# An encoder layer on one core: the mixer starts with the values' projection, the gates ride on it

## The chip, the core and the metric

The kernel runs on one NeuronCore of a Trainium2 chip. The core has five engines that run side by side, each with its own queue of instructions: TensorE (PE; matrix products, with a separate row PEld for loading the stationary operand), VectorE (DVE), ScalarE (ACT), GpSimd (POOL) and SyncE (SP), which here issues the DMAs. An instruction starts when it is at the head of its engine's queue and what it waits for has come. Products land in PSUM, eight banks of 128 x 512 float32; everything else lives in SBUF. The metric is the time of one execution on the device in microseconds (us).

## What is computed

One layer over a sequence of 512 tokens with 1024 features, all float32: a gated feed-forward block (FFN), a mixer, a second FFN, each between two normalizations and added to the residual.

```python
def reference(x, ...):
    h = swiglu(rmsnorm(x, norm_ffn1_pre), w_ffn1_in, w_ffn1_out)
    x = x + 0.5 * rmsnorm(h, norm_ffn1_post)
    h = mixer(rmsnorm(x, norm_mix_pre), w_mix_in, ...)
    x = x + rmsnorm(h, norm_mix_post)
    h = swiglu(rmsnorm(x, norm_ffn2_pre), w_ffn2_in, w_ffn2_out)
    return x + 0.5 * rmsnorm(h, norm_ffn2_post)

def mixer(xn, w_in, ...):
    bg, cg, hc, q, k, v, o, ig, fg = jnp.split(xn @ w_in, split_points, axis=-1)
    y_conv = bg * (conv3(cg * hc) + conv_b)
    li = ig + gate_i_bias
    lf = log_sigmoid(fg + gate_f_bias)
    h = mlstm(q, k, v, li, lf) + flip(mlstm(flip(q), flip(k), flip(v), ...))
    y_mlstm = sigmoid(o) * headnorm(h)
    return concatenate([y_conv, y_mlstm]) @ w_out
```

`xn @ w_in` has these columns: three blocks of 512 for the convolution, 256 queries, 256 keys, 512 values, 512 output gates and 16 scan gates (an input and a forget gate for each of 4 heads and 2 directions). The mLSTM is evaluated in four chunks of 128 tokens, with running sums and maxima over the forget gates inside and across chunks.

## The kernel before

**Precision.** A float32 operand is split into a rounded part `hi` and a rest `lo` (`split`, L291: a cast on ScalarE, L292, and a subtraction, mostly on VectorE, L294). A product is three matmuls, hi\*hi, hi\*lo and lo\*hi. So a contraction over 1024 features, eight blocks of 128, is 24 matmuls. The larger products of the FFNs use a seven-product (Strassen) scheme.

**Buffers.** `bigt` gives wide tiles (128 x 4 x 516) out of a pool of 13, `wpool` split weights (12 tiles, that is six pairs), `rawp` four weights as loaded, `ps` the eight PSUM banks. The weights form one list, `stream`; `w_load` loads the next of it, `w_split` splits it, and `w_get(ahead)` hands out the oldest pair and has up to `ahead` more split.

**Order.** The program is written in Python and traced; a planner then sets the order of each engine's queue, from the order of the source as priority and from its own estimate of when inputs and buffers are there. `pin` and `queued` keep an instruction in the order of the source. `tc.issue_after(ins)` puts instructions of a block behind `ins` on the queue of that instruction's engine, with no wait of its own.

**Around the change.** The first FFN ends with a loop over four token blocks `tb`: the last five blocks of hidden columns are multiplied (`mm_out`, L589), then `finish1(tb, acc)` adds the residual (`post_norm`, L398 and L406) and normalizes for the mixer (`pre_norm`, L383). For blocks 2 and 3 it does both after block 3. `flip` (L387) transposes a normalized block on PE (L391) into `xT`, features by tokens, and splits it (four `bigt` tiles in all). `within1` flips blocks 0 and 1 in the loop, inside the multiplications of blocks 2 and 3. In the middle of the FFN's output product `wgates` (L696) loads the 16 gate columns and spreads them on GpSimd over a zeroed tile, 32 apart, as hi and lo (L700, L706, L707).

The mixer then runs in this order:

1. Five jobs of `mm_cols` (L422): the spread gates and the four tiles of queries and keys, first over tokens 0 to 255, with `flip(2)` before the third job and `flip(3)` within the fifth, then over tokens 256 to 511. All these are 256 columns wide. ScalarE scales and copies queries and keys to `qk`.
2. The scan gates' chain, `chain1` to `chain4` (L780 to L841), on VectorE and ScalarE with 36 rows in use, while PE makes three output gate tiles with `col()` (512 wide, 24 matmuls each); `gate_o` applies the sigmoid.
3. The keys' transposes `pkn` (L869), the last output gate tile, `conv(0)`, and the transposes `pn1` and `pn2` of the chain's results (L902 to L905), copied to `nat1` and `nat2`.
4. The values by token blocks (L959): 24 matmuls of 512 columns for each block, the block of `xT` as the stationary operand. After the first, `weigh_k` (L928) multiplies keys by decay factors into `kp`, and `weigh_q` (four matmuls L942, eight products L948) does so for the queries.
5. `head_a(0)` (L997, L1004), `states` (L977), and the heads, with convolution tiles among them; then the output projection (L1113) and the second FFN.

Of the kernel before, what the change touches and what calls it, by code (L numbers as in the profile page):

```python
# [37 lines left out]
def encoder_kernel(ctx: ExitStack, tc: tile.TileContext, a: dict, out: bass.AP):
# [239 lines left out]
    nc.gpsimd.memset(warm, 0.0)
# [18 lines left out]
    def rstd(parts, n, mul, tag="rs"):  # L297
# [12 lines left out]
        nc.gpsimd.tensor_tensor(out=r[:, 0:w], in0=acc, in1=nhalf[:, 0:w], op=ALU.pow)  # L310
# [383 lines left out]
    wg = {}  # L694

    def wgates():  # L696
        raw = small.tile([P, KD, 16], F32, tag="rawg", name="rawg", bufs=1)
# [4 lines left out]
        rv = raw.rearrange("p k (q h) -> p k q h", h=4)
        hv = hi.rearrange("p k (q h) -> p k q h", h=32)
        lv = lo.rearrange("p k (q h) -> p k q h", h=32)
        for q in range(4):
            nc.gpsimd.tensor_copy(out=hv[:, :, q, 0:4], in_=rv[:, :, q, :])  # L706
            nc.gpsimd.tensor_tensor(out=lv[:, :, q, 0:4], in0=rv[:, :, q, :], in1=f32(hv[:, :, q, 0:4]), op=ALU.subtract)  # L707
# [4 lines left out]
    def finish1(tb, acc):  # L712
# [29 lines left out]
    qk = bigt()  # L742
    nc.scalar.mul(qk[:, 0, 0:512], pq0, DK ** -0.5)
    nc.scalar.mul(qk[:, 1, 0:512], pq1, DK ** -0.5)
    nc.scalar.copy(qk[:, 2, 0:512], pk0)
    nc.scalar.copy(qk[:, 3, 0:512], pk1)


    RA, RB = bigt(), bigt()
    nc.gpsimd.memset(RA[0:36, 0:2], 0.0)  # L750
    I, F = RA[0:36, 0, 0:512], RA[0:36, 1, 0:512]
    T1, T2 = RA[0:36, 2, 0:512], RA[0:36, 3, 0:512]
    B, A = RB[0:36, 0, 0:512], RB[0:36, 1, 0:512]
# [402 lines left out]
```

## Time and profile before

| what | us |
|---|---|
| median of 3 runs (916.7 to 917.62) | 917.5 |
| the profiled execution | 914.88 |
| its span, first to last instruction | 913.1 |
| first FFN's input and output products end, on PE | 353.2 |
| first head matmuls (L997) on PE | 438.1 |
| output projection (L1113) begins on PE | 519.8 |

The profile is of one execution, and times within it are counted from the span's start. Rows of groups give line, engine, operation, output and input tile, shapes, count, then busy time and mean ns of one, then the engine's idle time just before them and what ended it. Rows of stretches give for each engine its busy time and count of instructions, then the granted PE clock, the share of the DMA engines in use and GB/s. Rows of the timeline give start, duration, engine, line, operation and count, with idle time before and its releaser in brackets. An instruction's duration on PE is longer than the distance to the next one, as matmuls are pipelined; prices of matmuls are therefore taken from stretches.

### The profile page before, as it was taken

The numbers are of one execution on the slowest core, as the hardware profiler recorded it, in microseconds if no ns is written. First come the engines' busy times: TensorE is split into PE (matmuls) and PEld (weight loads), VectorE is DVE, ScalarE is ACT, GpSimd is POOL, SyncE is SP. The second block draws the span as 40 slices with busy tenths as digits, with TensorE's granted clock in tenths as the row PEclk, the third lists the DMA queues.
The fourth block names the chain that finished last, engine by engine and source line by source line (L and its number), as shares of the span: only waits on it lengthen the run. The fifth ranks groups of instructions, "written<-read, shape, count | busy, mean of one in ns | idle before, by whom it ended". The sixth has DMA issues, their size and how long they took to land.

```text
span 913.1 us, 15007 instructions
## 1 busy us (share of the span) xinstructions
PE 900.1 (99%) x6015; PEld 816.9 (89%) x6015; DVE 690.5 (76%) x1116; ACT 462.2 (51%) x802; POOL 44.9 (5%) x67
## 2 busy tenths in 40 slices
PE   9999999999999999999999999999999999999997
PEld 7999999999877888988888888999999999977885
DVE  6988998888988359474566647889888988999435
ACT  7655555555456225481655435545545545566311
POOL 5000000000002001000011000000000000000000
PEclk9999999999999999999999999999999999999999
DMA  8234443343235614231422602224443432443402
GB/s 262 62 116 113 120 134 99 100 129 97 90 130 148 201 47 116 58 96 56 116 71 70 204 4 75 65 70 117 115 117 94 121 108 84 123 138 110 162 2 91
DMA packets 126256, 96.47 MB, mean 106 GB/s; under 512 B 4181, under 2 KB 114793, under 8 KB 126186
## 3 DMA queue, kind: packets, MB, share of 16 engines
q1 hardware_dynamic: 126186, 95.51, 34.8%
q8 instruction: 47, 0.77, 0.3%
q14 instruction: 23, 0.19, 0.1%
HBM read 93.40 MB, written 2.10 MB: 105 GB/s over the span
## 4 chain that ended last, share of the span: by engine, by line
PE 95%; DVE 2%; ACT 1%; issue 0%; DMA 0%; POOL 0%; DVEq 0%; POOLq 0%; SPq 0%; ACTq 0%
PE ps L431 43%; PE ps L589 14%; PE ps L422 12%; PE ps L564 10%; PE ps L453 5%; PE ps L1113 5%; PE ps L959 2%; PE ps L1028 1%; DVE big L294 1%; PE ps L343 1%; DVE wlo L294 1%; PE ps L391 0%; PE ps L1036 0%; DVE big L531 0%; PE ps L977 0%
## 5 line engine op out<-in xcount | busy, mean ns | idle before, releaser
L294 DVE TENSOR_TENSOR wlo<-raw,whi 128x1024 fp32r<-128x1024 f32 x207 | 245.1, 1193 | 68.0 <-ACT whi L292 49.8
L292 ACT CAST whi<-raw 128x1024 fp32r<-128x1024 f32 x211 | 211.7, 1028 | 133.1 <-DVE raw L158 46.4
L431 PE MATMUL ps<-big,whi 128*128 128x256 f32 x1920 | 265.0, 280 | 0.0
L431 PEld LDWEIGHTS ps<-big,whi 128*128 128x128 f32 x1920 | 243.5, 188 | 1.0 <-ACT whi L292 0.4
L431 PE MATMUL ps<-big,wlo 128*128 128x256 f32 x960 | 150.9, 280 | 0.0
L431 PEld LDWEIGHTS ps<-big,wlo 128*128 128x128 f32 x960 | 129.3, 188 | 0.0
L589 PE MATMUL ps<-whi,big 128*128 128x512 f32 x384 | 121.9, 395 | 0.2 <-ACT whi L292 0.2
L589 PEld LDWEIGHTS ps<-whi,big 128*128 128x128 f32 x384 | 72.1, 188 | 17.5 <-ACT whi L292 0.7
L422 PE MATMUL ps<-big,whi 128*128 128x512 f32 (+1 forms) x384 | 79.8, 358 | 0.0
L564 PE MATMUL ps<-whi,big 128*128 128x512 f32 x240 | 76.0, 395 | 2.6 <-ACT big L292 2.6
L589 PE MATMUL ps<-wlo,big 128*128 128x512 f32 x192 | 75.6, 395 | 0.0
L422 PEld LDWEIGHTS ps<-big,whi 128*128 128x128 f32 x384 | 63.5, 188 | 10.7 <-issue 0.2
L431 PE MATMUL ps<-big,ws 128*128 128x256 f32 x480 | 65.3, 280 | 0.0
L431 PEld LDWEIGHTS ps<-big,ws 128*128 128x128 f32 x480 | 60.3, 188 | 0.0
L564 PEld LDWEIGHTS ps<-whi,big 128*128 128x128 f32 x240 | 44.7, 188 | 13.5 <-ACT big L292 3.4
L501 ACT COPY t<-ps 128x256 f32<-128x256 f32 x40 | 14.9, 371 | 72.2 <-PE ps L431 72.0
L292 ACT CAST big<-big 128x512 fp32r<-128x512 f32 (+2 forms) x68 | 36.1, 581 | 23.2 <-DVE big L531 10.8
L564 PE MATMUL ps<-wlo,big 128*128 128x512 f32 x120 | 44.9, 393 | 0.0
L589 PEld LDWEIGHTS ps<-wlo,big 128*128 128x128 f32 x192 | 36.1, 188 | 8.4
L422 PE MATMUL ps<-big,wlo 128*128 128x512 f32 (+1 forms) x192 | 41.1, 356 | 0.0
L294 DVE TENSOR_TENSOR big<-big,big 128x512 fp32r<-128x512 f32 (+2 forms) x68 | 40.8, 638 | 0.1
L422 PEld LDWEIGHTS ps<-big,wlo 128*128 128x128 f32 x192 | 32.1, 188 | 5.5
(212 smaller groups left out, 1135.0 us busy)
## 6 DMA issues: line engine op xcount, KB each, us to landing
raw<-in_w_ffn_in_dram SPq DMA_DIRECT2D x88, 512.0 KB, 4.8
raw<-in_w_ffn_out_dram SPq DMA_DIRECT2D x44, 512.0 KB, 4.5
raw<-in_w_mix_in_dram SPq DMA_DIRECT2D x24, 512.0 KB, 4.5
raw<-in_w_mix_out_dram SPq DMA_DIRECT2D x8, 512.0 KB, 3.7
raw<-in_w_ffn_out_dram SPq DMA_DIRECT2D x10, 256.0 KB, 3.7
out_dram<-x SPq DMA_DIRECT2D x8, 256.0 KB, 2.0
x<-in_x_dram SPq DMA_DIRECT2D x4, 256.0 KB, 4.3
x<-in_x_dram SPq DMA_DIRECT2D x2, 512.0 KB
```

Source lines behind the costliest of these rows:

```text
L292: latest["hi"] = nc.scalar.copy(out=hi, in_=src)
L294: latest["lo"] = eng.tensor_tensor(out=lo, in0=src, in1=f32(hi), op=ALU.subtract)
L343: pin(nc.tensor.transpose(out=pt[:, blk(k)], in_=xs[:, blk(4 * b + k)], identity=ident))
L422: nc.tensor.matmul(o, ww[:, k, :], xk(xT, xx, k, sl), start=n == 0, stop=n == 3 * KD - 1)
L431: pin(nc.tensor.matmul(o, ww[:, k, :], x[xx][:, k, :], start=first and n == 0, stop=n == 11, skip_group_check=True))
L453: pin(nc.tensor.matmul(o, ww[:, k, :], xq_hl(xq, (k // 4, th))[xx][:, k % 4, :], start=n == 0, stop=n == 3 * KD - 1))
L501: nc.scalar.copy(a_[:, h1], x[:, h0])
L564: nc.tensor.matmul(acc[tb + t][half], left[n][x][:, blk(t)], right[n][y], start=first and x == y == 0, stop=last_ and x == 1, skip_group_c ...
L589: nc.tensor.matmul(acc[tb][half], hT[hh][:, blk(tb)], w[ww][:, blk(half, 512)], start=fresh and hh == ww == 0, stop=k == NF - 1 and hh == ...
L959: nc.tensor.matmul(pv_, xk(xT, xx, k, blk(tb)), ww[:, k % 2, :], start=n == 0, stop=n == 3 * KD - 1)
L1028: nc.tensor.matmul(dest[d][c], E[:, d * 512 + c * P:d * 512 + (c + 1) * P], vv[:, c, h, :], start=c % 2 == 0, stop=before[d][c] < 0, skip_ ...
L1113: nc.tensor.matmul(acc[half], yy[yi][:, k % 4, blk(tb)], wmo[k][wi][:, blk(half, 512)], start=(n == 0 and yi == 0 and wi == 0), stop=(n == ...
```

## The change

The order of the mixer's first half is turned around.

- The values come first, by token blocks, with the 16 gate columns appended: wide tiles grow to 528 columns (`BW`), each of four holding hi and lo of two feature blocks of 512 value and 16 gate columns. `v_split` fills them, through the new hook `prep`, just ahead of the FFN's last loop. Each block takes 24 matmuls of 256 and 24 of 272 columns into two banks. `flip(2)` and `flip(3)` stand halfway in the tiles of blocks 1 and 2.
- The gate columns of a block are copied, 32 apart, into `spread`, and four transposes bring them to the layout that the chain reads (`pg`). The zeroed wide tile of `wgates`, its GpSimd writes and the gates' 48 matmuls go; `wgates` only loads the raw columns.
- `finish1` handles block 2 before block 3.
- Queries and keys are four `col()` tiles 512 wide (`project`), among the steps of the chain; the first two weights' splits are queued behind the last flip's, and the chain's GpSimd memsets behind the last power function of the norms.
- Two output gate tiles follow within the chain, then `pkn`, `pn1` and `pn2`, the third output gate tile, `weigh_k`, the fourth, `weigh_q`, and `conv(0)`.
- Some constants share storage: the warm-up operand with the raw gates, `ones` with `vrows`, `parl` with a part of `QT` (filled by GpSimd).

```diff
@@ weights in the order of loading
         if w_in is w2i:
+            stream += [(wm[blk(i, 2 * P), V0:V0 + 512].rearrange("(k p) f -> p k f", p=P), 2) for i in range(4)]
             stream += [cols(wm, c) for c in (Q0, Q0 + P, K0, K0 + P)]
             stream += [cols(wm, O0 + i * P) for i in range(4)]
             stream += [cols(wm, CG)]
-            stream += [(wm[blk(i, 2 * P), V0:V0 + 512].rearrange("(k p) f -> p k f", p=P), 2) for i in range(4)]
@@ def ffn(...)
+        if prep:
+            prep()
         for tb in range(NT):
...
     def wgates():
-        raw = small.tile([P, KD, 16], F32, tag="rawg", name="rawg", bufs=1)
-        queued(raw, wm[:, GT:GT + 16].rearrange("(k p) f -> p k f", p=P))
-        gt = bigt(F32R).rearrange("p q f -> p (q f)")
-        nc.gpsimd.memset(f32(gt[:, 0:2048]), 0.0)
...
+        queued(rawg, wm[:, GT:GT + 16].rearrange("(k p) f -> p k f", p=P))
+
+    def v_split():
+        for i in range(4):
+            if not loaded:
+                w_load(1)
+            (raw,), _ = loaded.pop(0)
+            bt = bigt(F32R).rearrange("p q f -> p (q f)")
+            hi, lo = (bt[:, blk(n, 2 * BW)].rearrange("p (k f) -> p k f", k=2) for n in range(2))
+            split(hi[:, :, 0:512], lo[:, :, 0:512], raw.rearrange("p (k f) -> p k f", k=2))
+            rg = rawg[:, 2 * i:2 * i + 2, :]
+            nc.gpsimd.tensor_copy(out=hi[:, :, 512:BW], in_=rg)
+            nc.gpsimd.tensor_tensor(out=lo[:, :, 512:BW], in0=rg, in1=f32(hi[:, :, 512:BW]), op=ALU.subtract)
+            wv.append((hi, lo))
@@ def finish1(tb, acc)
-        for b in {0: (0,), 1: (1,), 2: (), 3: (2, 3)}[tb]:
+        for b in {0: (0,), 1: (1,), 2: (2,), 3: (3,)}[tb]:
@@ the mixer's beginning
-    pg, pq0, pq1, pk0, pk1 = pts = [ps() for _ in range(5)]
-    jobs = [wg[0]] + [w_get(min(2, 3 - i)) for i in range(4)]
-    hooks = {(2, 0): lambda: flip(2, st[2], xT), (4, 2): lambda: flip(3, st[3], xT)}
-    for half in range(2):
-        for i, (pt, w) in enumerate(zip(pts, jobs)):
-            mm_cols(pt[:, blk(half, 256)], w, xT, blk(half, 256), hooks if half == 0 else None, i)
...
+    for tb in range(NT):
+        pv_ = [ps(), ps()]
+        n = 0
+        for k in range(KD):
+            hi, lo = wv[k // 2]
+            if (tb, k) in ((1, 4), (2, 4)):
+                flip(tb + 1, st[tb + 1], xT)
+            for xx, ww in ((0, hi), (0, lo), (1, hi)):
+                for i, at in enumerate((slice(0, 256), slice(256, BW))):
+                    nc.tensor.matmul(
+                        pv_[i][:, 0:at.stop - at.start], xk(xT, xx, k, blk(tb)), ww[:, k % 2, at],
+                        start=n == 0, stop=n == 3 * KD - 1)
+                n += 1
+        for i in range(2):
+            nc.scalar.copy(vv[:, tb, 2 * i:2 * i + 2, 0:DV], pv_[i][:, 0:256].rearrange("p (h e) -> p h e", e=DV))
+        nc.scalar.copy(spread_v[:, tb, :, 0:4], pv_[1][:, 256:272].rearrange("p (q h) -> p q h", h=4))
+    pg = ps()
+    for tb in range(NT):
+        nc.tensor.transpose(out=pg[:, blk(tb)], in_=spread[:, blk(tb)], identity=ident)
+    mark.update(latest)
+    with tc.issue_after(mark["lo"].ins), tc.issue_after(mark["hi"].ins):
+        w_split(2)
+    with tc.issue_after(mark["pow"].ins):
+        RA, RB = bigt(), bigt()
...
@@ behind the definitions
+    def project(i):
+        pt = col()
+        nc.scalar.mul(qk[:, i, 0:512], pt, DK ** -0.5 if i < 2 else 1.0)
+
+    chain1()
+    project(0)
+    project(1)
+    chain2()
+    project(2)
+    project(3)
+    chain3()
+    po.append(col())
+    chain4()
+    po.append(col())
+    gate_o(0)
+    gate_o(1)
...
+    po.append(col())
+    gate_o(2)
+    weigh_k()
+    po.append(col())
+    gate_o(3)
+    weigh_q()
+    conv(0)
```

The transposes `pkn`, `pn1` and `pn2` with their copies are moved without a change, other than `parl`'s place; the values' loop of before (L959, 512 columns wide) is removed.

More of the change, by code (lines that the diff above doesn't have):

```diff
@@ L58, in bigt @@
     def bigt(dt=F32):
-        return big.tile([P, 4, 516], dt, tag="big", name=nm("big"))
+        return big.tile([P, 4, BW], dt, tag="big", name=nm("big"))
     def ps():
@@ L276, in encoder_kernel @@
     nc.gpsimd.memset(nhalf, -0.5)
-    warm = const.tile([P, 256], BF16, name="warm")
+    rawg = const.tile([P, KD, 16], F32, name="rawg")
+    warm = rawg.rearrange("p k f -> p (k f)").bitcast(BF16)
     nc.gpsimd.memset(warm, 0.0)
-    ones = const.tile([1, P], F32, name="ones")
+    vrows = const.tile([20, P], F32, name="vrows")
+    ones = vrows[0:1, :]
     nc.gpsimd.memset(ones, 1.0)
@@ L433, in mm_part, with ffn @@
                 n += 1
-    def ffn(xq, between, finish, mid=None, within=None, ahead=(2, 2, 1, 1), late=None):
+    def ffn(xq, between, finish, mid=None, within=None, ahead=(2, 2, 1, 1), late=None, prep=None):
         h = [bigt() for _ in range((NF + 3) // 4)]
@@ L742, in encoder_kernel @@
[L742 to L753, printed above, removed]
-    CM, U = RB[0:36, 2, 0:512], RB[0:36, 3, 0:512]
-    nc.gpsimd.memset(U, 1.0)
@@ L892, in conv @@
             split(yc[0][:, i, 0:512], yc[1][:, i, 0:512], acc)
-    po.append(col())
-    gate_o(3)
-    conv(0)
-    pn1, pn2 = ps(), ps()
-    pn2v = pn2[:, 0:256].rearrange("p (c r) -> p c r", r=64)
-    for c in range(NT):
-        nc.tensor.transpose(out=pn1[:, blk(c)], in_=Q1[:, blk(c)], identity=ident)
-    for c in range(NT):
-        nc.tensor.transpose(out=pn2v[:, c, 0:36], in_=Q2[:, blk(c)], identity=ident[0:36, 0:36])
-    nc.tensor.matmul(
-        pn2[:, 256:272], parl.rearrange("p e x -> p (e x)"), acd.rearrange("p q c -> p (q c)"),
-        start=True, stop=True,
-    )
-    Ct = bigt()
-    Cf = Ct.rearrange("p q f -> p (q f)")
-    Cs = Cf[:, 0:12 * 129].rearrange("p (q i e) -> p q i e", q=4, i=3)
-    nat1 = Cf[:, 1552:2064].rearrange("p (c r) -> p c r", r=P)
-    nc.scalar.copy(nat1, ch(pn1))
-    nat2 = const.tile([P, NT, 36], F32, name="nat2")
-    nc.scalar.copy(nat2, pn2v[:, :, 0:36])
-    acb = const.tile([P, 4, 4], F32, name="acb")
-    nc.scalar.copy(acb.rearrange("p q c -> p (q c)"), pn2[:, 256:272])
     kpt = bigt()
@@ L949, in weigh_q @@
             qt_pair[pr] = qt
-    wv = [w_get(min(2, 3 - i)) for i in range(4)]
-    for tb in range(NT):
-        pv_ = ps()
-        n = 0
-        for k in range(KD):
-            hi, lo = wv[k // 2]
-            for xx, ww in ((0, hi), (0, lo), (1, hi)):
-                nc.tensor.matmul(pv_, xk(xT, xx, k, blk(tb)), ww[:, k % 2, :], start=n == 0, stop=n == 3 * KD - 1)
-                n += 1
-        nc.scalar.copy(vv[:, tb, :, 0:DV], pv_.rearrange("p (h e) -> p h e", e=DV))
-        if tb == 0:
-            weigh_k()
-            weigh_q()
+    po = []
+    qk = bigt()
+    def project(i):
[13 more added lines that the diff above has]
+    gate_o(1)
+    pkn = [ps(), ps()]
+    for c in range(NT):
+        for pr in range(2):
+            nc.tensor.transpose(
+                out=pkn[c // 2][:, blk(2 * (c % 2) + pr)], in_=qk[:, 2 + pr, blk(c)], identity=ident,
+            )
+    pn1, pn2 = ps(), ps()
+    pn2v = pn2[:, 0:256].rearrange("p (c r) -> p c r", r=64)
+    for c in range(NT):
+        nc.tensor.transpose(out=pn1[:, blk(c)], in_=Q1[:, blk(c)], identity=ident)
+    for c in range(NT):
+        nc.tensor.transpose(out=pn2v[:, c, 0:36], in_=Q2[:, blk(c)], identity=ident[0:36, 0:36])
+    nc.tensor.matmul(
+        pn2[:, 256:272], parl, acd.rearrange("p q c -> p (q c)"),
+        start=True, stop=True,
+    )
+    Ct = bigt()
+    Cf = Ct.rearrange("p q f -> p (q f)")
+    Cs = Cf[:, 0:12 * 129].rearrange("p (q i e) -> p q i e", q=4, i=3)
+    nat1 = Cf[:, 1552:2064].rearrange("p (c r) -> p c r", r=P)
+    nc.scalar.copy(nat1, ch(pn1))
+    nat2 = const.tile([P, NT, 36], F32, name="nat2")
+    nc.scalar.copy(nat2, pn2v[:, :, 0:36])
+    acb = const.tile([P, 4, 4], F32, name="acb")
+    nc.scalar.copy(acb.rearrange("p q c -> p (q c)"), pn2[:, 256:272])
+    po.append(col())
[5 more added lines that the diff above has]
+    conv(0)
     ym = (bigt(F32R), bigt(F32R))
```

74 lines of the change are left out of this document (30 added, 44 removed).

## The prediction

> **What bounds the kernel now.** I read the page's busy times first, then the list of who waited for whom with TensorE (PE) as the waiting engine, then busy times by stretch of the mixer's beginning, and last the timeline around its one hole.
>
> ```profile
> PE 900.1 (99%) x6015; PEld 816.9 (89%) x6015; DVE 690.5 (76%) x1116; ACT 462.2 (51%) x802; POOL 44.9 (5%) x67
> ...
> PE 95%; DVE 2%; ACT 1%; issue 0%; DMA 0%; POOL 0%; DVEq 0%; POOLq 0%; SPq 0%; ACTq 0%
> ```
>
> The first line is busy time by engine, the second the chain that ended last. Both name PE, from its first matmul to its last. So a microsecond saved on another engine is worth nothing unless PE waits for it, and one of PE's queue is worth a microsecond. Where does PE wait?
>
> ```profile
> PE ps L564 <- ACT big L292: 2.6, 2, 1.3
> PE ps L285 <- POOL warm L278: 1.3, 1, 1.3
> PE ps L391 <- DVE t L383: 1.0, 1, 1.0
> ```
>
> (Total us, times, longest.) Of the longer waits only L391, the transposes of `flip`, lies in the stage that is changed. The stage in stretches that I cut at the borders between matmul groups:
>
> ```profile
> core 0: us, PE busy (x) PEld busy (x) DVE busy (x) ACT busy (x) POOL busy (x), PEclk, DMA share, GB/s
> 353.17:358.84 5.67, 5.67 (x49) 5.61 (x47) 5.46 (x11) 3.20 (x9) 0.30 (x1) 1.00 0.81 229
> 358.84:360.02 1.18, 0.15 (x2) 0.03 (x1) 0.89 (x2) 0.00 (x0) 0.77 (x2) 1.00 0.96 234
> 360.02:370.74 10.72, 10.72 (x90) 10.37 (x90) 5.51 (x11) 3.60 (x8) 3.81 (x7) 1.00 0.08 29
> 370.74:384.95 14.21, 14.21 (x122) 14.21 (x121) 8.14 (x11) 5.37 (x7) 0.00 (x0) 1.00 0.18 43
> 384.95:401.63 16.68, 16.68 (x74) 13.47 (x73) 13.45 (x23) 14.16 (x17) 0.62 (x2) 1.00 0.42 124
> 401.63:402.43 0.80, 0.80 (x9) 0.79 (x8) 0.77 (x2) 0.79 (x1) 0.00 (x0) 1.00 0.15 26
> 402.43:413.61 11.18, 11.18 (x51) 9.05 (x50) 4.14 (x6) 9.02 (x13) 0.00 (x0) 1.00 0.41 115
> 413.61:414.71 1.10, 1.10 (x11) 0.90 (x9) 0.84 (x1) 0.90 (x2) 0.00 (x0) 1.00 0.81 243
> 414.71:438.12 23.41, 23.41 (x101) 18.72 (x100) 10.86 (x18) 5.50 (x10) 0.00 (x0) 1.00 0.11 30
> ```
>
> The reader should see that PE is full (clock 1.00) in every row but the second. In order the rows are: gates and first query tile over tokens 0 to 255; the hole; the two late flips and the rest of that half; the same five jobs over tokens 256 to 511; three output gate tiles; key transposes; the fourth gate tile and `conv(0)`; transposes of the decay factors; the values with `weigh_q`'s four matmuls in them. The counts take in instructions that straddle a border, so matmuls are counted from the code. The prices: a narrow matmul (256 columns) in the fourth row, 5 x 24 of them, is 14.21 / 120 = 0.1184 us. A wide one (512) in the fifth, 3 x 24, is 16.68 / 72 = 0.2317 us. A transpose in the sixth is 0.80 / 8 = 0.10 us.
>
> **Part by part.**
>
> *Gates' own projection goes.* 24 narrow matmuls for each half of the tokens, 48 x 0.1184 = 5.68 us, all on PE's path. **-5.68.**
>
> *Values narrow instead of wide.* Before: 96 wide, 23.41 - 4 x 0.2317 for `weigh_q` = 22.48 us. After: 96 of 256 columns and 96 of 272 (16 gate columns behind the values). No row has 272 columns. Between the two prices a column costs (0.2317 - 0.1184) / 256 = 0.00044 us, so 272 cost 0.1184 + 16 x 0.00044 = 0.1255 us. Ends: 0.1184 (the columns hide behind the weight load) and 0.2317 (as the next wider row). I take 0.1255, since 272 is sixteen columns from the first row and 240 from the second. 96 x 0.1184 + 96 x 0.1255 = 23.42 us. **+0.94**, with ends of +0.25 and +11.1.
>
> *Queries and keys wide instead of narrow.* 192 x 0.1184 = 22.73 against 96 x 0.2317 = 22.24. **-0.49.**
>
> *Gates turned.* Gates now come out by tokens, so four transposes of `spread` are added, 4 x 0.10. **+0.40.** They wait for ScalarE's three copies out of the last value tile. From the nearest rows:
>
> ```profile
> L501 ACT COPY t<-ps 128x256 f32<-128x256 f32 x40 | 14.9, 371 | 72.2 <-PE ps L431 72.0
> ...
> 414.99 0.18 ACT L917 COPY acb<-ps 128x16 f32<-128x16 f32 x1
> ```
>
> 2 x 0.37 + 0.18 = 0.92 us. If the first query tile's matmuls (24 x 0.2317 = 5.6 us, needing only `xT` and a split weight) stand ahead of the transposes on PE's queue, this is hidden. If not, some 1 us shows. Ends 0 and 1.0; I take **+0.3**. Queued behind them is all of PE.
>
> *The hole.* It is the wait for block 2's norm:
>
> ```profile
> 347.76 1.22 DVE L294 TENSOR_TENSOR wlo<-raw,whi 128x1024 fp32r<-128x1024 f32 x1
> ...
> 351.79 1.22 DVE L294 TENSOR_TENSOR wlo<-raw,whi 128x1024 fp32r<-128x1024 f32 x1
> ...
> 355.92 1.22 DVE L294 TENSOR_TENSOR wlo<-raw,whi 128x1024 fp32r<-128x1024 f32 x1
> ...
> 359.13 1.41 DVE L383 SCALAR_TENSOR_TENSOR t<-x,rs,gb 128x512 f32<-128x512 f32 x2 [0.39 <-POOL rs L310]
> ...
> 364.17 1.42 DVE L383 SCALAR_TENSOR_TENSOR t<-x,rs,gb 128x512 f32<-128x512 f32 x2 [0.73 <-POOL rs L310]
> ```
>
> Five weight splits (three shown) of queries, keys and the first output gate stand on VectorE's (DVE) queue among the norms of blocks 2 and 3, whose last steps are the L383 rows. After the change PE has value tiles of blocks 0 and 1 first. A tile is 24 x 0.1184 + 24 x 0.1255 = 5.85 us, so `flip(2)`, halfway in tile 1, is due at 353.17 + 5.85 + 2.93 = 361.95, and `flip(3)` after two more half tiles and one flip, at 368.6. Even at today's times the norms end at 360.5 and 365.6, 1.4 and 3.0 us earlier. The query splits also leave that place (they are queued behind the last flip), and block 2's norm is issued one block earlier. **-1.03** (1.18 less 0.15 busy). What is late next is the last flip's own split:
>
> ```profile
> L292 ACT CAST whi<-raw 128x1024 fp32r<-128x1024 f32 x211 | 211.7, 1028 | 133.1 <-DVE raw L158 46.4
> ...
> L294 DVE TENSOR_TENSOR big<-ps,big 128x512 fp32r<-128x512 f32 x24 | 15.6, 684 | 16.1 <-ACT big L292 16.1
> ...
> L292 ACT CAST big<-ps 128x512 fp32r<-128x512 f32 x24 | 13.5, 588 | 25.9 <-PE ps L343 15.3 <-PE ps L391 10.3
> ```
>
> Cast 0.59 and subtract 0.68 for each half stand against 2.9 us of matmuls between the flip and its first reader. (The first row is the cast of a weight, used below.)
>
> *What moves off PE.* The values' four splits go ahead of the FFN's last blocks, one cast and one subtract each:
>
> ```profile
> 306.60:346.60 40.00, 40.00 (x178) 32.42 (x177) 19.00 (x33) 10.52 (x24) 2.20 (x4) 1.00 0.27 81
> ...
> 283.48 2.04 POOL L706 CAST big<-rawg 128x32 fp32r<-128x32 f32 x4 [12.27 <-DMA rawg<-in_w_mix_in_dram]
> 285.48 3.27 POOL L707 TENSOR_TENSOR big<-rawg,big 128x32 fp32r<-128x32 f32 x4
> 332.44 0.55 POOL L310 TENSOR_TENSOR rs<-rs,nhalf 128x1 f32<-128x1 f32 x1 [43.69 <-DVE rs L306]
> ...
> 306.61 132.69 SPq L147 DMA_DIRECT2D raw<-in_w_mix_in_dram  x22
> ...
> raw<-in_w_mix_in_dram SPq DMA_DIRECT2D x24, 512.0 KB, 4.5
> ```
>
> DVE is busy 19.0 of these 40 us, and gets 4 x 1.22 = 4.9 more. GpSimd keeps its four casts and four subtracts of the same size, 5.3 us in an idle stretch of 43.69. Without that cover a norm's power function would queue behind them and its flip come up to 5.3 us late. The four value loads take the queries' places on SP's queue; at 4.5 us each one after another they land by 306.6 + 18 = 325, and are read at 353. The other loads keep their count. `weigh_k` and `weigh_q` keep their instructions and have two column tiles and `conv(0)` as cover where they had three value tiles. I cost all this at nothing. The VectorE copy of `parl` and one GpSimd memset, off the path, go for nothing as well.
>
> *Sum:* -5.68 + 0.94 - 0.49 + 0.40 + 0.3 - 1.03 = -5.56, say **-5.6 us**. The profiled execution took 914.88 us, so 909.3; the median of the runs shown is 917.5, 2.6 above it, and so 911.9 is my time.
>
> **A rule weighed.** The row says 0.1184 us for 256 columns and 0.2317 for 512: by the column nearly the same. The Trainium skill, TensorE: Matmul & The Clock Gate, section "Back-to-back issue gap", gives for streams of loads and matmuls about 81 ns at 128 columns and 131 ns at 512, which makes wide ones much cheaper by the column. An estimate on that line, 98 ns at 256 and 100 at 272, makes the values 96 x 0.131 = 12.6 us before and 19.0 after, +6.4 instead of +0.94, and the change no gain. The trace disagrees with it at 512 columns (231.7 ns against 131).
>
> **Rivals.**
>
> *A hole stays at the mixer's start* (-2.6, 914.9 us). There are 13 wide buffers. By the code's lifetimes the FFN's last blocks hold five (two for sums, three for hidden columns), `xT` four, and the values' weights now four: exactly 13. If the fourth weight must wait for the FFN's sums, last read here,
>
> ```profile
> 357.65 0.68 DVE L398 TENSOR_TENSOR t<-big,gb 128x512 f32<-128x512 f32 x1
> ```
>
> it is split at 358.3 + 1.03 + 1.22 = 360.6, while PE wants it after 36 matmuls, at 357.6: 3.0 us lost. For it: no buffer is spare. Against: VectorE frees those sums earlier without the splits.
>
> *It doesn't do what it says* (917.5). The queue order isn't the source's but comes from a planner with estimated times. If PE's queue has a group ahead of a flip or of the gates' transposes that in truth comes later, waits like the 1.03 us recur, and some five of these eat the gain. For it: the hole before is such a wait. Against: in 85 us there is just one.
>
> *The gate chain ends last* (slower). The gates' scan runs on VectorE and ScalarE from the first row here to the end of the second, and the third reads its result:
>
> ```profile
> 379.09 3.04 DVE L783 TENSOR_SCALAR big<-ps,gbias 4x512 f32<-4x512 f32 x4
> ...
> 405.50 1.40 DVE L834 TENSOR_TENSOR big<-big,big 4x512 fp32r<-4x512 f32 x2 [1.64 <-ACT big L833]
> ...
> 413.61 0.60 PE L902 MATMUL ps<-ident,big 128*128 128x128 f32 x4
> ```
>
> 27.8 us, with 6.7 to spare. Afterwards gates exist only when the last value tile is done: 353.17 + 23.4 + two flips and a small transpose 1.8 = 378.4, copies and transposes to 379.7. PE then has six column tiles (33.4), and key transposes: the reader is due at 378.4 + 0.4 + 33.4 + 0.8 = 413.0. Spare 5.5. Each us of chain beyond 33.3 costs one; from 38.9 on the change is slower. At 41 it is +2.1: 919.6. Against: the splits per column tile stay, and the sigmoids, which stood within the chain, are now issued behind it.
>
> *Narrow matmuls paced by their loads* (slower). PEld's mean is 188 ns for each load; were that the pace, 192 x (0.188 - 0.122) = +12.7, net +7.1: 924.6. Against: the first stretch has 48 narrow ones, each with its load, in 5.67 us. The skill's rule above would also end on this side.
>
> **How the numbers follow.** Forecast 0.64, hole 0.17, no effect 0.08, chain 0.08, load pace 0.03. The best case is 272 columns at the price of 256 and no wait for the copies, -5.56 - 0.68 - 0.3 = -6.5 (911.0), and the three runs of before differ by 0.9 us; low end 909.6. The upper end has to reach past the hole's 914.9 with the same scatter: 916.2. That leaves out the last three cases, 0.19. This kernel's measurement tells about 0.2% (1.8 us) from no change; faster than that are the forecast and the hole, 0.81; the same 0.08; slower 0.11.
>
> **What would show it.** Right: no 256-column `L422` matmuls in the mixer; value tiles at about 5.85 us each; no PE wait for L383 near 360; PE's first head matmuls (438.1 before) near 432.5, and everything behind shifted by that. Wrong: value tiles over 6.5 us (272 columns dear); PE idle before the gates' transposes over 1 us; a PE wait for a flip, or for a value weight's split; PE idle ahead of the transposes of the decay factors (chain). The forecast falls if the stretch to the first head matmul shrinks by 5.6 us but a later one grows.

## The result and the profile after

The changed kernel takes 911.0 us (median of 6 runs, 909.44 to 911.71) against 916.78 of the kernel before, run beside it (6 runs, 914.57 to 917.62): a ratio of 0.9938, with a 95% interval of 0.9927 to 0.995. That is 5.78 us less, where 5.56 had been worked out. Its profiled execution took 911.16 us.

The page after, with the busy times by engine and the chain that ended last:

```profile
PE 896.4 (99%) x5971; PEld 814.5 (90%) x5971; DVE 691.1 (76%) x1115; ACT 460.2 (51%) x807; POOL 42.5 (5%) x68
...
PE 91%; DVE 4%; DMA 2%; ACT 1%; issue 1%; DVEq 0%; POOLq 0%; POOL 0%; ACTq 0%
```

PE is still the bound, with 44 matmuls fewer: 48 of the gates are gone and four transposes have come. The list of PE's waits after (total us, times, longest):

```profile
PE ps L567 <- ACT big L295: 2.7, 2, 1.3
PE ps L567 <- ACT wt L295: 2.0, 2, 1.0
PE ps L288 <- POOL rawg L280: 1.3, 1, 1.3
PE ps L592 <- ACT whi L295: 0.4, 2, 0.2
PE ps L434 <- ACT whi L295: 0.2, 1, 0.2
```

The wait for block 2's norm is not among them (the transposes of `flip` are now L394), and none of these is in the mixer. The wait for `wt` was one of 0.9 us before; it lies in the first FFN's output product and is taken up below. The mixer's first stage, cut at the borders between groups of matmuls:

```profile
core 0: us, PE busy (x) PEld busy (x) DVE busy (x) ACT busy (x) POOL busy (x), PEclk, DMA share, GB/s
356.51:365.25 8.74, 8.74 (x74) 8.73 (x73) 6.61 (x14) 3.56 (x11) 3.48 (x6) 1.00 0.01 3
365.25:366.04 0.79, 0.79 (x11) 0.79 (x9) 0.00 (x0) 0.16 (x1) 0.79 (x2) 1.00 0.00 0
366.04:381.69 15.65, 15.65 (x132) 15.65 (x130) 8.13 (x9) 8.28 (x15) 1.11 (x3) 1.00 0.31 84
381.69:382.17 0.48, 0.48 (x6) 0.28 (x4) 0.40 (x1) 0.14 (x1) 0.00 (x0) 1.00 1.15 299
382.17:415.76 33.59, 33.59 (x146) 27.17 (x146) 22.97 (x35) 22.75 (x31) 0.62 (x2) 1.00 0.47 125
415.76:417.74 1.98, 1.98 (x19) 1.78 (x17) 1.23 (x1) 1.06 (x2) 0.00 (x0) 1.00 0.27 79
417.74:428.96 11.22, 11.22 (x49) 9.13 (x49) 3.30 (x7) 3.16 (x6) 0.00 (x0) 1.00 0.33 93
428.96:429.89 0.93, 0.93 (x5) 0.75 (x4) 0.67 (x1) 0.60 (x1) 0.00 (x0) 1.00 0.00 0
429.89:435.56 5.67, 5.67 (x25) 4.33 (x24) 5.52 (x9) 1.05 (x1) 0.00 (x0) 1.00 0.34 95
```

The rows are: 72 value matmuls; `flip(2)`; 120 value matmuls with `flip(3)` and one of the gates' transposes; two more of these and a small one of L875; six column tiles with the fourth gates' transpose; key transposes and those of the chain's results; two output gate tiles; `weigh_q`'s matmuls; `conv(0)`. In all nine PE is busy as long as the stretch lasts. The stage took 79.05 us, from the end of the FFN's products at 356.51 to the first head matmul at 435.56; before it was 353.17 to 438.12, 84.95 us. **5.90 us are gone from this stage**, and the prediction's 5.56 had named this stage alone.

The spans of the two profiled executions (913.1 and 909.4) differ by 3.7 only, because they started differently. The first matmul of the first FFN ran at 10.75 us in the one before and at 13.70 in the one after. Other runs of both families began at times between these two, so lengths of stages are compared from here on, and not instants.

### The profile page after: what moved, and what is told of

The parts are those of the page before. It is cut to its first block, busy times and chain, and to the rows that moved or that the text cites. A ratio compares the mean times of both kernels' runs of the same rounds, so it can differ in the third digit from the quotient of the medians.

```text
span 909.4 us, 14920 instructions
## 1 busy us (share of the span) xinstructions
PE 896.4 (99%) x5971; PEld 814.5 (90%) x5971; DVE 691.1 (76%) x1115; ACT 460.2 (51%) x807; POOL 42.5 (5%) x68
## 4 chain that ended last, share of the span: by engine, by line
PE 91%; DVE 4%; DMA 2%; ACT 1%; issue 1%; DVEq 0%; POOLq 0%; POOL 0%; ACTq 0%
PE ps L434 39%; PE ps L592 13%; PE ps L425 12%; PE ps L567 9%; PE ps L456 5%; PE ps L1133 5%; PE ps L755 3%; DMA raw<-in_w_ffn_in_dram 2%; DVE big L297 1%; DVE wlo L297 1%; PE ps L346 1%; PE ps L1048 1%; DVE big L534 1%; ACT big L295 1%; PE ps L288 1%
## 5 line engine op out<-in xcount | busy, mean ns | idle before, releaser
L297 DVE TENSOR_TENSOR wlo<-raw,whi 128x1024 fp32r<-128x1024 f32 x203 | 240.0, 1192 | 49.3 <-ACT whi L295 25.7
L295 ACT CAST whi<-raw 128x1024 fp32r<-128x1024 f32 x207 | 207.4, 1029 | 123.6 <-DVE raw L159 48.1
L434 PEld LDWEIGHTS ps<-big,whi 128*128 128x128 f32 x1920 | 243.0, 188 | 1.2 <-ACT whi L295 0.7
L434 PEld LDWEIGHTS ps<-big,wlo 128*128 128x128 f32 x960 | 129.5, 188 | 0.0
L425 PE MATMUL ps<-big,whi 128*128 128x512 f32 x320 | 78.3, 397 | 0.0
L567 PE MATMUL ps<-whi,big 128*128 128x512 f32 x240 | 75.2, 392 | 2.7 <-ACT big L295 2.7
L425 PEld LDWEIGHTS ps<-big,whi 128*128 128x128 f32 x320 | 59.5, 188 | 13.7 <-issue 0.2
L567 PEld LDWEIGHTS ps<-whi,big 128*128 128x128 f32 x240 | 44.7, 188 | 12.9 <-ACT big L295 3.5
L567 PE MATMUL ps<-wlo,big 128*128 128x512 f32 x120 | 44.6, 391 | 0.0
L425 PE MATMUL ps<-big,wlo 128*128 128x512 f32 x160 | 40.4, 395 | 0.0
L425 PEld LDWEIGHTS ps<-big,wlo 128*128 128x128 f32 x160 | 30.0, 188 | 7.0
```

Source lines behind the costliest of these rows:

```text
L295: latest["hi"] = nc.scalar.copy(out=hi, in_=src)
L297: latest["lo"] = eng.tensor_tensor(out=lo, in0=src, in1=f32(hi), op=ALU.subtract)
L425: nc.tensor.matmul(o, ww[:, k, :], xk(xT, xx, k, sl), start=n == 0, stop=n == 3 * KD - 1)
L434: pin(nc.tensor.matmul(o, ww[:, k, :], x[xx][:, k, :], start=first and n == 0, stop=n == 11, skip_group_check=True))
L567: nc.tensor.matmul(acc[tb + t][half], left[n][x][:, blk(t)], right[n][y], start=first and x == y == 0, stop=last_ and x == 1, skip_group_c ...
```

## The experiments

My theory was the prediction's sum: less work in PE's queue and one hole closed. Against it stood four rivals: that the new order of the queue is all that counts, that some buffer or norm holds PE at the start, that the gate chain sets the end, and that the mixed widths cost or save something else. All stage lengths below are read from the traces, between the same two matmuls as above. A kernel that was timed several times has its ratio to the kernel before with its interval; of the others, timed once, only the stages are compared (kernels that left the stage's work alone gave 79.05 to 79.06 in four executions).

| kernel | first FFN, us | stage, us | heads, us | second FFN to the end, us | time, us |
|---|---|---|---|---|---|
| before | 342.42 | 84.95 | 81.68 | 346.17 | 916.78 |
| after | 342.81 | 79.05 | 81.53 | 345.30 | 911.0 |
| e1_flip_later | 341.52 | 83.72 | 81.67 | 346.36 | 915.67 |
| e2_gates_one_product | 341.63 | 84.68 | 81.68 | 347.37 | 917.17 |
| e3_norms_late | 341.91 | 79.06 | 81.53 | 345.23 | 909.61 |
| e4_qk_halves | 342.84 | 79.37 | 81.53 | 345.27 | 910.8 |
| e5_values_512_and_16 | 342.60 | 88.49 | 81.53 | 345.23 | 917.37 |
| e6_one_more_wide_tile | 342.20 | 79.06 | 81.53 | 345.23 | 910.43 |
| e7_gates_not_riding | 342.55 | 78.50 | 81.54 | 345.23 | 907.79 |
| e8_chain_longer | 342.80 | 88.67 | 81.52 | 345.21 | 920.58 |
| e11_chain_half | 343.47 | 79.54 | 81.53 | 345.26 | 911.97 |
| e9_before_row528 | 341.07 | 85.06 | 81.81 | 345.17 | 915.2 |
| e10_after_row532 | 344.33 | 78.95 | 81.24 | 346.87 | 913.87 |
| again | 342.88 | 79.06 | 81.53 | 345.29 | 910.55 |

### The hole, closed by itself in the kernel before

```diff
-    hooks = {(2, 0): lambda: flip(2, st[2], xT), (4, 2): lambda: flip(3, st[3], xT)}
+    hooks = {(3, 0): lambda: flip(2, st[2], xT), (4, 2): lambda: flip(3, st[3], xT)}
```

> The kernel before, with the flip of block 2 ahead of the fourth of the five narrow jobs instead of the third, so that PE has 24 more narrow matmuls (2.84 us) ahead of it. My theory (two terms: PE work removed, and the hole of 1.03 us closed): PE's wait for L383 near 360 us goes, and the stretch from the end of the FFN's products to the first head matmuls shrinks from 84.95 to about 83.9 us; the time falls by 1.0 us. Rival (the gain is all one of order, of norms and flips that come earlier): about 5 us less, near 80 us. Second rival (a wait only moves): 84.95 stays, with PE waiting elsewhere in the stretch.

The stage shrank from 84.95 to 83.72, by 1.23, and the ratio is 0.9988 [0.9979, 0.9998]. The wait for L383 is not in its list of waits any more:

```profile
PE ps L564 <- ACT big L292: 2.6, 2, 1.3
PE ps L285 <- POOL warm L278: 1.3, 1, 1.3
PE ps L564 <- ACT wt L292: 0.9, 1, 0.9
```

So one more query job ahead of the flip covers the norm, and the hole was worth a fifth of the change. The rival that closing it is all the change does falls: 4.7 us of the stage are left to explain.

### The gates' matmuls, a third of them kept

```diff
...
-        for ww, xx in ((hi, 0), (hi, 1), (lo, 0)):
+        for ww, xx in ((hi, 0), (hi, 1), (lo, 0))[:terms]:
...
@@ the mixer's beginning
-            mm_cols(pt[:, blk(half, 256)], w, xT, blk(half, 256), hooks if half == 0 else None, i)
+            mm_cols(pt[:, blk(half, 256)], w, xT, blk(half, 256), hooks if half == 0 else None, i, 3 if i else 1)
```

This is the kernel before with the gates computed from hi\*hi alone: 32 matmuls leave, 32 x 0.1184 = 3.79 us.

> The kernel before, with the gates' projection cut to its first product (hi*hi, 16 of 48 narrow matmuls; the two other products of the gates are left out). My theory: PE work falls by 32 x 0.1184 = 3.79 us, but 16 of these matmuls were cover for the flip of block 2, so the hole grows by up to 1.9 us, from 1.0 to about 2.9; the stretch shrinks from 84.95 to about 83.1 us. Rival (gates' work is hidden and only order counts): the stretch stays at 84.9 or grows by the hole. If the hole does not grow: about 81.2.

It brought almost nothing: the stage took 84.68, 0.27 less, where 83.1 had been expected, and the ratio is 0.9998 [0.9988, 1.0008]. The timeline of PE at the hole (start, duration; in brackets the idle time and who ended it) shows why:

```profile
361.90 1.23 PE L391 MATMUL ps<-ident,t 128*128 128x128 f32 x8 [2.91 <-DVE t L383]
362.89 3.38 PE L422 MATMUL ps<-big,whi 128*128 128x256 f32 x16
366.06 1.45 PE L422 MATMUL ps<-big,wlo 128*128 128x256 f32 x8
367.35 2.05 PE L422 MATMUL ps<-big,whi 128*128 128x256 f32 x16
369.24 1.11 PE L422 MATMUL ps<-big,wlo 128*128 128x256 f32 x8
```

The hole grew from 1.03 to 2.91 us. That takes back 16 matmuls' worth, as expected. But the 24 matmuls behind it need 367.35 - 362.89 = 4.46 us, and the next 24, of the same shapes, 370.19 - 367.35 = 2.84 (the next group starts at 370.19). Stretches of the same place, cut where the granted clock changes, have the reason in their column PEclk (the last but two):

```profile
358.90:361.90 3.00, 0.09 (x1) 0.03 (x1) 2.50 (x8) 0.00 (x0) 1.06 (x2) 1.00 0.92 253
361.90:363.37 1.47, 1.47 (x12) 1.29 (x13) 1.47 (x3) 0.79 (x2) 0.00 (x0) 1.00 0.52 202
363.37:366.78 3.41, 3.41 (x18) 3.41 (x18) 2.52 (x7) 1.73 (x5) 1.31 (x2) 0.50 0.03 5
366.78:370.19 3.41, 3.41 (x31) 3.41 (x30) 0.69 (x2) 0.00 (x0) 2.51 (x6) 1.00 0.00 0
```

From 1.47 us behind the idle time on, the clock is granted at 0.50 for 3.41 us, and the 24 matmuls take 4.46 - 2.84 = 1.62 us more. A hole of 2.9 us thus cost 4.5, while the one of before, in a stretch of 1.18 with clock 1.00 around it, cost only itself. The sum closes: 3.79 us of matmuls less, 1.88 of hole and 1.62 of slow clock more make 0.29, and 0.27 were measured. Removing PE work ahead of a transpose that waits for another engine buys nothing; the change was right to put other matmuls there as well.

### Three details of the new order

```diff
@@ e3: the norm of block 2 behind block 3 again
-        for b in {0: (0,), 1: (1,), 2: (2,), 3: (3,)}[tb]:
+        for b in {0: (0,), 1: (1,), 2: (), 3: (2, 3)}[tb]:
@@ e4: queries and keys in halves of 256 columns
-        pt = col()
+        pt, ww = ps(), w_get()
+        for half in range(2):
+            mm_cols(pt[:, blk(half, 256)], ww, xT, blk(half, 256))
@@ e6: one more wide tile, held until the gates are copied
+    held = []
+
     def v_split():
+        held.append(bigt())
+        nc.gpsimd.memset(held[0][:, 0, 0:16], 0.0)
...
         nc.scalar.copy(spread_v[:, tb, :, 0:4], pv_[1][:, 256:272].rearrange("p (q h) -> p q h", h=4))
+    nc.scalar.copy(held[0][:, 0, 0:16], pv_[1][:, 256:272])
```

> The changed kernel with block 2's norm done after block 3's products, as before. My theory: the flip of block 2 is covered by a value tile and a half; its norm may come 3 us later than the 358.0 us of the changed kernel's trace and is still ahead of the flip at 365.2; no PE wait, 79.05 us stays within 0.2. Rival (the earlier norm is what closed the hole): a wait of about 1 us or more for L386 at the flip.

> The changed kernel with the four query and key tiles made in two halves of 256 columns each, as before. My theory: 192 x 0.1184 against 96 x 0.2317, +0.49 us; the stretch grows from 79.05 to about 79.5 us. Rival (paced by 188 ns of weight load): 192 x (0.188 - 0.118) = +13 us. If the wide form gave nothing: 79.05.

> The changed kernel with one further wide tile in use from the values' splits until the last value tile is copied (two small writes to it), that is 14 wanted at a time where 13 exist. By the rival of the buffers (exactly 13 are in use at the mixer's start): the tile that comes last waits for the FFN's sums, and PE idles about 3 us at the start of the values; the stretch grows to about 82. My theory: the kernel has no buffer to spare there either, so some wait of 0 to 3 us; if none shows, the count of 13 was too high.

The order of the norms in the source makes no difference (79.06), but e3 did not delay the norm: the planner kept its place on VectorE's queue. It begins 0.11 us behind the stage's start in e3 (355.18 against 355.07) and 0.13 in the kernel after, so e3 says nothing about a late norm. That PE comes late enough is read from the timelines. After, the norm of block 2 is done at 356.64 + 1.41 = 358.05, and its transposes run at 365.25, behind one and a half value tiles; even the norm of before, done 7.4 us after the stage's start, would be 1.4 us ahead of a flip 8.7 us after it.

```profile
356.64 1.41 DVE L386 SCALAR_TENSOR_TENSOR t<-x,rs,gb 128x512 f32<-128x512 f32 x2
...
365.25 1.03 PE L394 MATMUL ps<-ident,t 128*128 128x128 f32 x8
...
387.15 0.27 PE L764 MATMUL ps<-ident,t 128*128 128x128 f32 x1
...
387.53 3.04 DVE L804 TENSOR_SCALAR big<-ps,gbias 4x512 f32<-4x512 f32 x4 [3.11 <-PE ps L764]
...
407.67 1.26 ACT L842 ACTIVATE big<-big 4x512 f32<-4x512 f32 x2
...
410.48 1.40 DVE L855 TENSOR_TENSOR big<-big,big 4x512 fp32r<-4x512 f32 x2
...
416.64 0.60 PE L960 MATMUL ps<-ident,big 128*128 128x128 f32 x4
417.17 0.43 PE L962 MATMUL ps<-ident,big 36*128 36x36 f32 x4
```

(The rows from 387.15 on are used further down.)

Queries and keys in halves cost 0.32 us (79.37), where 0.49 was the difference of the two prices. One wide tile more leaves the stage at 79.06 and adds no wait of PE in it. It is felt, though: in e6 GpSimd waits for wide buffers, which it does not in the kernel after (two of three such waits):

```profile
POOL big L790 <- PE ps L759: 11.6, 1, 11.6
POOL big L714 <- PE ps L567: 9.1, 2, 8.8
```

So the pool of 13 is in full use, as the rival had it, but its time was wrong: it had the fourth value weight split until 360.6, and in the kernel after that split ends at 323.71 + 1.23 = 324.94, 31.6 us ahead of the values. Such leads cover the waits for a buffer.

### What the riding gate columns cost, and what a matmul of their own would

```diff
@@ e7: the gate columns are not multiplied
-                for i, at in enumerate((slice(0, 256), slice(256, BW))):
+                for i, at in enumerate((slice(0, 256), slice(256, 512))):
...
@@ e5: 512 value columns, and 16 gate columns by themselves
-                for i, at in enumerate((slice(0, 256), slice(256, BW))):
+                for i, at in enumerate((slice(0, 512), slice(512, BW))):
...
```

The lines left out read the copies from the new places.

In the first kernel the gates are not computed: the chain is fed with value columns, so that only the 16 columns on 96 matmuls are missing.

> The changed kernel with the values' second matmul 256 columns wide instead of 272: the gate columns are not multiplied, and the chain is fed value columns in their place. My theory (a column costs 0.00044 us): 96 x 0.0071 = 0.68 us less in the values, the stretch from the end of the FFN's products to the first head matmuls falls from 79.05 to about 78.4 us. Rival (a narrow matmul is paced by its weight load, so columns hide behind it): no difference, 79.0. Second rival (272 is dear): more than 1.5 us less.

> The changed kernel with each pair of value matmuls cut as 512 and 16 columns instead of 256 and 272; same products. My theory: the wide ones cost 0.234 us as in the old loop; the 16 columns wide ones, each with a load of its own, cost what a matmul of few columns costs in this kernel, from 0.07 (129 columns on half the rows, 12 in 0.87 us) to 0.10 us (a transpose), so 96 x (0.234 + 0.07 to 0.10 - 0.244) = +5.8 to +8.6 us on the stretch of 79.05. Rival (a 16-column matmul costs only its columns, 0.007 us): -0.3 us. Rival by the skill's rule (wide matmuls far cheaper by the column, 131 ns at 512): 96 x (0.131 + 0.08 - 0.2) = about +1 us.

Without the columns the stage takes 78.50, 0.55 less, or 0.0057 us for 16 columns on a matmul. As 96 matmuls of their own they cost 9.44 us more than in the kernel after (88.49). The groups of L755 in that kernel, by shape:

```profile
L755 PE MATMUL ps<-big,big 128*128 128x512 f32 x96 | 33.3, 477 | 0.0
L755 PE MATMUL ps<-big,big 128*128 128x16 f32 x96 | 16.5, 171 | 0.0
```

The pair of 512 and 16 columns costs (9.44 / 96) + 2 x 0.1224 = 0.343 us. The 0.1224 is the mean distance after: (8.74 + 14.76) / 192, with `flip(3)` and one small transpose, 0.89, taken out of the third stretch. With a wide one at 0.2317, some 0.11 is left for 16 columns: nearly the 0.1184 of 256 columns. This is past the upper expectation of 8.6 by 0.8. So from 16 to 256 columns the width hardly counts. Each of these matmuls loads 128 stationary columns of its own, which would set such a floor; that is argued, since no run changed the load alone. The matmuls of `states` point the same way: they load 64 stationary columns and stream 129, and 48 of them take 2.79 us (437.31 to 440.10), 0.058 each. The Trainium skill, TensorE: Matmul & The Clock Gate, section "LDWEIGHTS (loading the stationary operand)", has a load take about P / 1.2 ns, 107 ns for 128 columns, and this trace agrees with its 0.11 us.

### The gate chain, made longer

```diff
     def chain2():
+        for _ in range(18):
+            nc.vector.tensor_tensor(out=F, in0=F, in1=F, op=ALU.min)
```

The extra steps are minima of a tile with itself, 18 in e8 and 9 in e11.

> The changed kernel with 18 further VectorE operations of 0.68 us (the minimum of the forget row with itself, which changes nothing) in the gates' chain, 12.2 us longer. The chain's results are read by the transposes L960 to L963 at 416.6 us, 4.8 us behind the chain's end at 411.9. Rival of the chain (each us beyond the spare costs one): +7.4 us, 86.5. My theory: the planner moves output gate tiles (5.56 us each, two stand behind those transposes) ahead of them, so that 0 to 2 us show.

> The changed kernel with 9 further operations in the gates' chain instead of 18, about half of the lengthening that made PE wait 6.9 us and brought the stretch to 88.7 us. By the count of the prediction (chain results 4.8 to 5.5 us ahead of their reader): 9 x 0.70 = 6.3 us leave a wait of 0.8 to 1.5 us at the transposes, 80 to 80.6 us. If the spare is what the longer chain implies (12.7 us longer gave 6.9 of wait, so 5.8 of spare): 0.5 us, 79.6. With no slow clock behind it, since the wait is short.

Each such step takes 0.68 us on VectorE. Eighteen steps made the stage 9.62 us longer (88.67), nine 0.49 (79.54). The waits of PE in the mixer of each, e8 first, then e11:

```profile
PE ps L962 <- issue: 6.1, 1, 6.1
...
PE ps L964 <- ACT big L844: 0.8, 1, 0.8
```

```profile
PE ps L964 <- ACT big L844: 0.4, 1, 0.4
```

To read the spare from this, one must know what the transposes read. L960 and L962 (two lines further in e8 and e11) read `Q1` and `Q2`, whose last writes are ScalarE's exponentials L841 and L842. L855, which the expectations and the prediction took for the chain's end, writes a row of results (`IHL`) that only `weigh_q` reads, at 428.96. In the kernel after, L842 ends at 407.67 + 1.26 = 408.93, and L962 runs at 417.17: **8.2 us to spare**. In e11 that exponential ends at 418.05, 8.7 us later when counted from the stage's start, and PE waits 0.4. In e8 it ends at 424.67, 15.7 us later, and the transposes of `Q2` run 7.5 us later. So both runs agree with a spare of 8.2. The steps alone (6.1 and 12.3 us) would give 5.7 and 5.4, but they did not come alone: two more weight splits of 1.2 us fell between the chain's operations on VectorE in e11, and three more in e8. I had also held that the planner would move tiles around a longer chain; it did not, and that theory falls.

PE waits 6.1 + 0.8 = 6.9 us in e8. The other 2.7 us of the 9.62 are explained by the clock, as the stretches of e8 show from the wait on:

```profile
416.70:422.80 6.10, 0.09 (x1) 0.00 (x0) 5.97 (x13) 3.81 (x6) 0.00 (x0) 0.70 0.30 86
422.80:425.70 2.90, 2.06 (x11) 1.66 (x11) 2.57 (x6) 2.84 (x6) 0.00 (x0) 0.50 0.00 0
425.70:429.50 3.80, 3.80 (x10) 3.02 (x10) 3.09 (x8) 1.10 (x4) 0.00 (x0) 0.52 0.00 0
429.50:433.00 3.50, 3.50 (x16) 2.82 (x15) 0.00 (x0) 1.62 (x2) 0.00 (x0) 1.00 0.00 0
```

Ten matmuls need 3.80 us at a clock of 0.52, and 16 need 3.50 at 1.00. The 0.70 and 0.52 are means: the clock is 1.00 until 419.1, 2.4 us into the wait, 0.50 from there to 429.35, and 1.00 again.

### Outside the stage: the rows of the wide tiles

The second FFN was not touched, yet from its first matmul to the end the kernel after takes 345.30 us and the one before 346.17. The wide tiles have grown from 516 to 528 columns, so the rows that PE reads are 2112 bytes long in place of 2064. To see whether that does it, e9 is the kernel before with wide tiles of 528 columns; since they need more room, it shares the constants' storage as the change does. And e10 is the kernel after with 532 (2128 bytes), where two small edits make the room.

```diff
@@ e9, in the kernel before
-        return big.tile([P, 4, 516], dt, tag="big", name=nm("big"))
+        return big.tile([P, 4, 528], dt, tag="big", name=nm("big"))
...
@@ e10, in the kernel after
-        return big.tile([P, 4, BW], dt, tag="big", name=nm("big"))
+        return big.tile([P, 4, 532], dt, tag="big", name=nm("big"))
...
-    junk = const.tile([P, D], BF16, name="junk")
+    junk = const.tile([P, 512], BF16, name="junk")
...
-        st1[tb] = pre_norm(tb, g_pre, 1)
+        st1[tb] = pre_norm(tb, g_pre, 2)
...
```

> The kernel before with wide tiles of 528 columns instead of 516 (rows of 2112 bytes instead of 2064), and the small constants stored as in the changed kernel to make room; nothing of the order is changed. Open is why the changed kernel's second FFN, in which no line is changed, takes 345.3 us from its first matmul to the end where the kernel before takes 346.2 to 346.4, and why 151 wide matmuls of the first FFN's last loop take 34.80 us instead of 35.16. Theory (the row length of the wide tiles sets it): second FFN near 345.3, these 151 matmuls near 34.8, and the time about 1 to 2 us below the kernel before. Rival (it comes from the planner's order): 346.2 and 35.16 stay.

> The changed kernel with wide tiles of 532 columns (rows of 2128 bytes, no multiple of 64 as 2112 is), and the squares of two early norms taken in two halves to make room. Theory of the row length (multiples of 64 bytes are read faster): the second FFN goes back to about 346.2 us and the 151 matmuls to about 35.2. Rival (any row other than 2064 will do, or order): 345.3 and 34.8 stay.

> The changed kernel unchanged, beside the kernel before and e9 on one chip: the time 0.994 of before; stretch 79.05, second FFN 345.3.

e9 is faster than the kernel before, 915.2 against 917.0, ratio 0.9979 [0.9969, 0.9989], with its stage unchanged (85.06). The kernel after, repeated beside it, took 910.55: ratio 0.9925 [0.9908, 0.9941]. In the chains of PE, a piece is start, duration, line and number of matmuls. Three unbroken pieces have the same shapes in every kernel. For before, e9 and e10:

```profile
306.87 35.16 PE ps L589 x151
...
591.97 190.76 PE ps L431 x1620
...
862.43 44.54 PE ps L589 x192
```

```profile
308.89 34.79 PE ps L591 x151
...
593.66 190.61 PE ps L433 x1620
...
863.44 44.22 PE ps L591 x192
```

```profile
312.01 34.85 PE ps L592 x151
...
590.45 191.51 PE ps L434 x1620
...
861.45 44.55 PE ps L592 x192
```

With 2112 bytes the wide matmuls run 1.1% and 0.7% closer together than with 2064. This repeats in the other kernels: the groups take 35.16 and 44.54 to 44.59 us in all three with 2064, and 34.79 to 34.80 and 44.21 to 44.22 wherever they are unbroken with 2112. The length of the whole second FFN is a weaker witness: in e2, with 2064 and no line of it changed, it is 347.37, 1.2 us more than before, 0.61 of this a wait at 813.89 that the kernel before has not. With 2128 the last group is as slow as with 2064 and the 1620 narrow ones are slower than in both, but the first group stays fast. So the storage does change PE's pace by up to 1%, and my rule for it, rows of a multiple of 64 bytes, is only half borne out. Which property of the addresses decides is open.

## Why the prediction was right

The time was right, and so was the place: the stage lost 5.90 us where the sum had 5.56. Term by term:

| term | predicted, us | shown, us | by |
|---|---|---|---|
| gates' own matmuls | -5.68 | not measured as a whole | e2: 32 of the 48 are worth about 3.8 (0.27 + 1.88 + 1.62) |
| values in two widths | +0.94 | +1.02 | 192 x 0.1224 against 22.48 |
| of these, the gate columns | +0.68 | +0.55 | e7 |
| queries and keys wide | -0.49 | -0.32 | e4 |
| four transposes | +0.40 | about +0.4 | not measured alone; two and L875's take 0.48 |
| wait for the copies | +0.3 | 0 | no idle PE in the stage |
| the hole | -1.03 | -1.23 | e1 |

The shown terms, with the gates and the transposes at the predicted price, add up to -5.81, and the stage has -5.90. The choice that mattered was the price of 272 columns: taken sixteen columns up the line from 256, not from the row of 512, where the change would have been a loss. e7 shows that price within 0.13 us over 96 matmuls. The wait for the copies was not paid, because the planner put the last gates' transpose into the first query tile: it runs at 387.15, behind some 21 matmuls of that tile.

Two steps of the prediction were wrong without harm, both about the gate chain. The chain was to start when the transposes are done, 26.5 us after the end of the FFN's products (379.7 on the clock of before); it started at 387.53, 31.0 after, by the same move. And its end was taken from the wrong row: L834 (L855 after) is not what the transposes read. Up to the exponentials that they do read (L821 before, L842 after) the chain takes 25.7 us before, from 379.09 to 404.82, and 21.4 after, from 387.53 to 408.93. Two sigmoids with their table loads stood within it on ScalarE's queue before and come behind it after. The spare, forecast as 5.5 us, is 8.2: the start came 4.5 us later, but the chain up to its true end is 6.4 us shorter than assumed, and the reader of `Q2` comes 0.8 later.

The rivals: a hole left at the start falls by the stretches (PE never idle there); the full pool that it rests on is real (e6), but the values' weights are split 31.6 us early. No effect falls by the ratio. The gate chain is a real mechanism that begins to cost when its exponentials come 8.2 us later, but my price for it, one us for each us, is too low: with a wait of 6.9 us each cost 9.62 / 6.9 = 1.4. Narrow matmuls paced by their loads at 0.188 us fall (0.1224 with a load each). What floor there is lies at 0.11, below what the kernel uses. The estimate from the Trainium skill's 131 ns for 512 columns (TensorE: Matmul & The Clock Gate, section "Back-to-back issue gap") was weighed for the values alone, and there it fails: +6.4 was estimated, and they cost 23.50 us in the new widths, gates included, against 22.48 in the old. That it makes the change no gain was a wrong sum: on the same line the queries and keys would change by 96 x 0.131 - 192 x 0.098 = -6.2 and the gates' going by -48 x 0.098 = -4.7, so this estimate too ends at a gain, of about 4.8 us.

What the prediction did not see lies outside the stage, and two things there work against each other. The new storage gave 917.0 - 915.2 = 1.8 us (e9; 1.0 to 2.8 by its interval). Against that the first FFN takes longer in the kernel after than in e9, 342.88 against 341.07. All of it arises ahead of the group of 151 matmuls, which begins 297.02 us behind the first FFN's first matmul in the repeated kernel (310.45 - 13.43) and 295.21 in e9 (308.89 - 13.68). About 1.2 us of the 1.81 are in waits: 2.0 us for ScalarE's casts into `wt` (L567 above), in two waits, one in each FFN, where e9 has this one, in the second, and 0.2 for the cast behind it:

```profile
PE ps L566 <- ACT wt L294: 1.0, 1, 1.0
```

Every kernel with the new order has these waits in the first FFN, and none with the old order. The rest of the 1.81 is within what the first FFN varies by from kernel to kernel (341.91 to 343.47 in those with the new order and 2112 bytes). That the planner, with other work in the mixer, orders ScalarE's casts in the FFN differently is what the traces suggest; which of the moved instructions does it was not tried. So the sum was right for its stage, and that the total came out close is in part luck: an unforeseen gain of about 1.8 met an unforeseen loss of 1.2 to 1.8.

## What to carry to other kernels

Where PE is full, count its queue: a small projection that rides as 16 extra columns on matmuls that run anyway cost 0.006 us each, where a matmul of its own cost about 0.11, nearly as much as one of 256 columns. Before removing PE work, look at what it was covering; a hole is closed by putting independent matmuls ahead of it, and the two long ones here, of 2.9 and 6.9 us, cost 4.5 and 9.6. Before calling an instruction the end of a chain, look up which tile its reader reads. And compare the stages that were not changed too: a new tile width or a new order can move the time there by as much as a term of the sum.

## What the hardware showed that was not expected

- **Idle time slows what follows.** After 2.91 us of idle PE the granted clock was 0.50 for 3.41 us, from 1.47 us behind the idle time on (e2); in a wait of 6.1 us it fell to 0.50 after 2.4 us and stayed there until 6.5 us behind the wait (e8). After 1.18 us (before) and 0.42 us (e11) it stayed at 1.00. The Trainium skill, TensorE: Matmul & The Clock Gate, section "What's actually happening", has the clock halve after an idle window of about 3.4 us; here idle times of 2.9 us and, up to the fall, 2.4 us sufficed. In both cases some 1 us of transposes lies next to the idle time; whether they count as idle no run here shows.
- **The pace of PE depends on where the tiles lie**, by up to 1%: 35.16, 34.79 and 34.85 us for the same 151 matmuls with rows of 2064, 2112 and 2128 bytes.
- **PE's beginning differs between executions.** The four small matmuls that start at 4.0 us took 2.01 us in the profile before and 3.78 in the one after, and the first FFN began at 10.74 to 13.70 us in kernels of both families. The stretches show a clock of 1.00 in both, but they do so wherever the trace has no record of the clock: the first record is at 4.10 us before and at 13.29 after. In the three executions whose record starts at 4.0 to 4.5 us these four matmuls took 1.98 to 2.21 us and the first FFN began at 10.74 to 11.28; in the other eleven, where it starts at 10.5 to 13.3, 3.78 and 13.09 to 13.70. That PE runs at a lower clock until the first record is what this suggests; no run shows it. Timeline rows of after:

```profile
4.01 3.78 PE L291 MATMUL ps<-g_row,vrows 1*128 1x512 f32 x4
...
13.70 0.51 PE L456 MATMUL ps<-big,whi 128*128 128x256 f32 x2
```
